# Values of the first two heads from the raw input in float32, with the norm's root and shift applied at read-out, in one step of a hybrid attention / mLSTM backbone

## The chip, the cores and the metric

The kernel runs on one core of a Trainium2 chip. The metric is device microseconds for one execution; three timed executions of the kernel before gave 2232.55, 2234.36 and 2235.95 us, median 2234.36. The engines are named as the profile names them: PE (matrix products), PEld (its weight loads), DVE, ACT and POOL (elementwise work), SP (which issues DMA transfers). L98 is line 98 of the kernel.

## The reference, cut to what matters

One layer is computed for 128 context tokens and 1024 latent tokens, 1152 in all, 1024 channels wide. Only its first stage is touched:

```
sh1, sc1, ... = adaln(cond, w_mod, b_mod)          # silu(cond) @ w_mod + b_mod; one set for the
h = rmsnorm(x, g_norm_mix) * (1.0 + sc1) + sh1     # context tokens, another for the latent ones
z = h @ w_in                                       # z is then split into q, kv, gates, values ...
mv = zmv.reshape(B, S, MLSTM_HEADS, MLSTM_DV)      # values: 4 heads of 256 columns
```

With r the reciprocal root of a token's mean square and A = g (1 + sc1) per channel, h = r x A + sh1. So a token's values can be had as h @ W, or as r (x @ (A W)) + sh1 @ W. Everything is float32.

## The kernel before, in words

Tokens lie in the columns: the input x is held as eight slices k of 128 channels, each in two halves j of 576 tokens; the 1152 tokens are also nine chunks c of 128. Chunk 0 holds the context tokens; chunk 4 lies across the two halves, and is copied together for the split products by `copy4`. Float32 products that matter are made of three products of a split operand (`mm3`, L98 to L100: high by high, high by low, low by high), after ACT has written the high part (`hi`, L69) and DVE the difference (`lo`, L75). Float32 products without a split are used where they are small.

`start` (L329 to L541) makes the normed and modulated h and the values of all heads, before `z_lat` begins the other projections from combinations of h (`t_ops`, L547 onward, makes those on POOL, ACT and DVE in the background). In order:

- `gemv` (L353): for three blocks of 256 channels, silu(c) times a block of `w_mod`, as eight float32 products with a stationary operand of two columns, then a transposition by four small products, then DVE writes shift `mod1` and scale `A1`. The last two channel slices get theirs by `row`: products and sums of rows on DVE, POOL and ACT.
- `stats` and `xr`: sum of squares per token (ACT and DVE), the reciprocal root by PE and DVE, spread over the partitions, and x times it, on DVE and POOL.
- `modk`: scale and shift (ACT for half 0, DVE for half 1), then the high and low parts.
- `vmm`: the values of one head are 256 columns, six chunks GA in the six PSUM banks named mm, then the three of GB. For each chunk and slice k three products of 256 columns, with the chunk of h stationary. `vout` copies a chunk's 256 columns out and stores them.

Each engine works through its own list of instructions in order. The lists come from the program's order by a scheduler that moves instructions by its own estimates. SP's list holds all loads and stores of this stage; a DMA whose buffer is not free holds up those behind it. Weights go through four buffers `wr` (raw) and four `wo` (high and low parts).

## Time and profile before

| what | value |
|---|---|
| median of 3 runs | 2234.36 us |
| the profiled execution | 2234.02 us |
| span of its trace (first to last instruction) | 2232.2 us |
| mean granted PE clock | 0.964 |
| PE busy | 2067.2 us (93%) |
| PEld busy | 1902.9 us (85%) |
| DVE busy | 1541.2 us (69%) |
| POOL busy | 1012.8 us (45%) |
| ACT busy | 927.0 us (42%) |

The page gives busy shares of the whole span, and then the span in forty slices of 55.8 us; the first three slices and a third of the fourth are `start`. A row of the timeline has a start, a time, the engine, the line, what is written from what, shapes and the number of instructions merged; the bracket is the idle time before it and what ended it. A PE product's time in a row is its latency; successive products overlap, so that their rate is read from starts or from merged rows. An unsplit float32 product is recorded as two.

### The profile page before, as it was taken

To read this page: it belongs to the slowest core of one execution; us is meant where nothing else is said; L and a number is where in the kernel's file an instruction comes from. 1 tells how busy PE (TensorE), PEld (TensorE's weight loads), DVE (VectorE), ACT (ScalarE), POOL (GpSimd) and SP (SyncE) were. 2 spreads that over 40 slices of the span, in tenths; PEclk is the share of its full clock that TensorE was granted. 3 is DMA by queue.
4 is the path that set the end of the run, shared out by engine and by line. 5 is a ranking of instruction groups with operands and counts; after the bars stand their busy time and mean duration, and the time that the engine had idled before them with its cause. 6 is when DMAs were issued, how large, how long until landed. Compare 5 with 4: busy or idle time off the path is not lost.

```text
span 2232.2 us, 37660 instructions
## 1 busy us (share of the span) xinstructions
PE 2067.2 (93%) x13913; PEld 1902.9 (85%) x13913; DVE 1541.2 (69%) x2710; ACT 927.0 (42%) x1846; POOL 1012.8 (45%) x754
## 2 busy tenths in 40 slices
PE   5799998999979987999999999889999999989897
PEld 1799998999978874667676799879999999989897
DVE  6735745988845877655665547899645555799895
ACT  4232333545545654333433335444322222356464
POOL 3712122767723523444445534677766634431501
PEclk8799999999999998999999999899999999999899
DMA  7221243555569876222224564224555522557664
GB/s 284 66 93 60 73 152 122 166 182 167 168 214 327 256 222 211 85 73 69 75 78 125 172 214 141 97 90 131 168 183 166 177 87 79 162 174 249 220 196 132
DMA packets 235671, 340.82 MB, mean 153 GB/s; under 512 B 20286, under 2 KB 171550, under 8 KB 234462
## 3 DMA queue, kind: packets, MB, share of 16 engines
q1 hardware_dynamic: 226942, 328.73, 46.3%
q0 software_dynamic: 4848, 6.06, 1.1%
q10 hardware_dynamic: 3696, 3.61, 0.5%
q8 instruction: 110, 1.80, 0.3%
q14 instruction: 75, 0.61, 0.1%
HBM read 250.55 MB, written 87.80 MB: 152 GB/s over the span
## 4 chain that ended last, share of the span: by engine, by line
PE 45%; DVE 12%; DMA 8%; POOL 6%; issue 5%; ACT 2%; SPq 1%; DVEq 0%; POOLq 0%; ACTq 0%
PE mm L98 11%; PE mm L100 11%; PE mm L99 10%; DVE wo L75 4%; DMA pr<-w_fo 3%; PE pv L1455 3%; PE st L98 2%; PE st L99 1%; PE st L100 1%; PE mx L1377 1%; DVE sm L1379 1%; PE p L1081 1%; POOL ps L1755 1%; POOL ps L1752 1%; POOL wm L701 1%
## 5 line engine op out<-in xcount | busy, mean ns | idle before, releaser
L100 PE MATMUL mm<-th,wo 128*128 128x288 f32 x1840 | 547.8, 298 | 14.5 <-DVE wo L75 14.2
L98 PE MATMUL mm<-th,wo 128*128 128x288 f32 x1840 | 548.9, 298 | 6.1 <-ACT m L1693 2.8
L99 PE MATMUL mm<-tl,wo 128*128 128x288 f32 x1840 | 547.3, 298 | 0.0
L100 PEld LDWEIGHTS mm<-th,wo 128*128 128x128 f32 x1840 | 349.9, 190 | 18.5 <-DVE wo L75 18.0
L75 DVE TENSOR_TENSOR wo<-wr,wo 128x512 fp32r<-128x512 f32 (+1 forms) x317 | 313.7, 1005 | 64.0 <-ACT wo L69 59.5
L98 PEld LDWEIGHTS mm<-th,wo 128*128 128x128 f32 x1840 | 349.0, 190 | 8.6 <-ACT m L1693 3.0
L99 PEld LDWEIGHTS mm<-tl,wo 128*128 128x128 f32 x1840 | 349.4, 190 | 0.1
L69 ACT ACTIVATE wo<-wr 128x512 fp32r<-128x512 f32 (+1 forms) x317 | 187.3, 608 | 147.6 <-PE mm L100 70.5
L75 DVE TENSOR_TENSOR wo<-ws,wo 128x512 fp32r<-128x512 f32 x188 | 185.8, 991 | 68.4 <-ACT wo L69 68.3
L69 ACT ACTIVATE wo<-ws 128x512 fp32r<-128x512 f32 x188 | 116.7, 627 | 276.4 <-PE mm L100 147.3
L1424 POOL TENSOR_TENSOR es<-es,p 128x512 f32<-128x512 f32 x112 | 157.3, 1404 | 91.3 <-ACT p L1417 87.4
L100 PE MATMUL mm<-xh,wo 128*128 128x288 f32 x616 | 183.5, 299 | 10.7 <-DVE wo L75 10.7
L98 PE MATMUL mm<-xh,wo 128*128 128x288 f32 x616 | 183.0, 297 | 1.2 <-ACT wo L69 1.2
L99 PE MATMUL mm<-xl,wo 128*128 128x288 f32 x616 | 183.8, 299 | 0.0
L1665 POOL TENSOR_TENSOR ws<-wr,ws 128x512 f32<-128x512 f32 x47 | 61.8, 1315 | 244.2 <-DVE wo L75 238.8
L1417 ACT ACTIVATE p<-st 128x512 f32<-128x512 f32 (+1 forms) x152 | 87.4, 578 | 157.7 <-PE st L100 146.5
L1379 DVE TENSOR_REDUCE sm<-mx 128x1 f32<-128x384 f32 (+1 forms) x200 | 99.1, 539 | 66.4 <-PE mx L1377 65.5
L98 PE MATMUL mm<-B,wo 128*128 128x288 f32 x456 | 134.8, 296 | 2.2 <-DVE zo L1681 1.3
L100 PE MATMUL mm<-B,wo 128*128 128x288 f32 x456 | 134.8, 296 | 0.0
L99 PE MATMUL mm<-B,wo 128*128 128x288 f32 x456 | 134.8, 296 | 0.0
L701 POOL TENSOR_TENSOR wm<-wm,sr 128x512 f32<-128x512 f32 x64 | 100.1, 1566 | 65.4 <-DVE mj L700 61.0
L100 PEld LDWEIGHTS mm<-xh,wo 128*128 128x128 f32 x616 | 117.2, 191 | 13.0 <-DVE wo L75 12.9
(430 smaller groups left out, 5272.7 us busy)
## 6 DMA issues: line engine op xcount, KB each, us to landing
wr<-w_ff SPq DMA_DIRECT2D x56, 512.0 KB
wm<-wm SPq DMA_DIRECT2D x32, 512.0 KB
wr<-d_w SPq DMA_DIRECT2D x32, 512.0 KB
d_z<-zo SPq DMA_DIRECT2D x48, 288.0 KB
d_g<-uu SPq DMA_DIRECT2D x44, 288.0 KB
wr<-w_big SPq DMA_DIRECT2D x24, 512.0 KB
wr<-w_fo SPq DMA_DIRECT2D x24, 512.0 KB
pr<-w_fo SPq DMA_DIRECT2D x40, 256.0 KB
```

Of the source, the lines that this page charges most:

```text
L69: i = self.nc.scalar.activation(out, in_, AF.Copy)
L75: return self.nc.vector.tensor_sub(out, in_, f32v(hi)).ins
L98: mm(out, lhs[0], rhs[0], start=first, stop=False)
L99: mm(out, lhs[0], rhs[1], start=False, stop=False)
L100: self.pe = mm(out, lhs[1], rhs[0], start=False, stop=last).ins
L701: nc.gpsimd.tensor_tensor(w[:, n], w[:, n], sr[:, 1], op=ALU.mult)
L1081: self.pe = mm(p1, A[:, h], V[:, h], start=True, stop=not carried).ins
L1379: self.iv = nc.vector.tensor_reduce(sm[:, t, j:j + 1], s[:, :kc], axis=AX.X, op=ALU.max, negate=True).ins
L1417: self.ia = nc.scalar.activation(p[:, :n], st[:, :n], AF.Exp).ins
L1424: nc.gpsimd.tensor_tensor(U["sum"], U["sum"], p, op=ALU.add)
L1455: self.pe = nc.tensor.matmul(pv[g * AV:(g + 1) * AV, q0:q0 + w], v[:, kb[c]], U["P"][c][:, q0:q0 + w], start=c < 2, stop=c == U["nc"] - 1, ...
L1665: G.tensor_tensor(s4, a12, s2, op=ALU.subtract)
```

## The change

In `start`:

- **First values from raw x.** The values of heads 0 and 1 of chunks 1 to 6 are made of x as it was loaded, unsplit, in float32 (`rawmm`), against weights that ACT multiplies by `A1` (L514). Chunk 4 is made as two products of 64 tokens each, written to the two halves of a bank's partitions, so that no copy is needed. `shift` multiplies the shift by the unscaled weights on PE (a stationary operand of 32 columns), `spread` copies the row over the partitions, and `vout` of these chunks does r times PSUM plus that row (L498).
- **Loads block by block.** Four blocks of `w_mod` (all 1024 channels) are loaded, each followed by a piece of `w_v` and two slices of x. The row products of the last two slices and their loads (`row`, `rload`, `rparams`, `sload`) are gone.
- **Modulation on column groups.** `gemv` has a stationary operand of 32 columns (two used), and four products write the four groups of 32 partitions of one bank; the sum of the groups is taken by the small products that transpose.
- **Two heads wide.** A value product has 512 columns in place of 256, and `vout` writes 512.
- **modk.** x times root and scale is one DVE instruction for slices 0 to 3 (L429), then ACT adds the shift; for slices 4 to 7 POOL multiplies by the root (L425) and ACT does scale and shift. It comes at the end of the raw products, since it overwrites x.
- The remaining values: heads 2 and 3 of GA = chunks 0 to 3, 5, 6 (while `modk` runs); then heads 0 and 1 of chunks 7, 8, 0; then heads 2 and 3 of 7, 8, 4, with `t_ops` in the background of the last two.

The instructions that follow `start` are the same on every engine, but for 25 places of PE and 16 of DVE where neighbours change places.

The first place is PE's list where the raw part ends (the names mm_209 to mm_220 are the six banks of the raw chunks; mx are the small results; wh, wl split weights; B_71, B_72 the high and low part of half 0, slices 0 to 3). Before, the split products follow the root's own small products:

```order
L280 MATMUL mm_327<-dg_324,ones 128x128 x2
L361 MATMUL mx_432<-ident,rows_430 128x2 x4
L280 MATMUL mm_334<-dg_331,ones 128x128 x2
L280 MATMUL mm_340<-dg_338,ones 128x64
L98 MATMUL mm_357<-wh_277,B_72_353 128x256
L99 MATMUL mm_357<-wl_278,B_72_353 128x256
L100 MATMUL mm_357<-wh_277,B_73_354 128x256
```

Now the same small products stand behind the last raw ones:

```order
L469 MATMUL mm_215<-ws_360,x_20_144 64x512
L473 MATMUL mm_218<-ws_360,x_20_144 128x512
L473 MATMUL mm_220<-ws_360,x_20_144 128x512
L418 MATMUL mx_397<-dg_396,ones 128x128 x4
L418 MATMUL mx_408<-dg_407,ones 128x128 x4
L418 MATMUL mx_419<-dg_418,ones 128x128
L481 MATMUL mx_459<-wr_175,shs 32x512 x2
L492 MATMUL mx_465<-shv,selr 128x512
L98 MATMUL mm_507<-wh_486,B_71_427 128x512
L99 MATMUL mm_507<-wl_487,B_71_427 128x512
L100 MATMUL mm_507<-wh_486,B_72_428 128x512
```

Between the last raw product and the first split one there are nine products that spread the root, three for the shift, and, on other engines, all that makes B.

The second place is DVE's list at that time (vs are the read-outs of raw banks, b12l the low parts of half 1, B_97 those of half 0, slices 4 to 7):

```order
L485 TENSOR_TENSOR shv<-shv,mx_459 64x512
L75 TENSOR_TENSOR B_72_428<-x_17_141,B_71_427 128x576
L75 TENSOR_TENSOR B_97_573<-x_19_143,B_96_572 128x576
L75 TENSOR_TENSOR B_72_428<-x_17_141,B_71_427 128x576 x3
L75 TENSOR_TENSOR B_97_573<-x_19_143,B_96_572 128x576
L75 TENSOR_TENSOR b12l<-x_18_142,b12h 128x576
L498 SCALAR_TENSOR_TENSOR vs_468<-mm_209,y_382,shv 128x512
L498 SCALAR_TENSOR_TENSOR vs_471<-mm_211,y_382,shv 128x512
L498 SCALAR_TENSOR_TENSOR vs_474<-mm_213,y_382,shv 128x512
L75 TENSOR_TENSOR b12l<-x_18_142,b12h 128x576
L75 TENSOR_TENSOR B_97_573<-x_19_143,B_96_572 128x576
L498 SCALAR_TENSOR_TENSOR vs_477<-mm_215,y_382,shv 128x512
```

The twelve L429 instructions stand just ahead of these rows; the first read-out of a raw bank is the twenty-first instruction, counted from the first L429.

The third place is POOL's list (t_118 is `t_ops`' first difference, c the copies for chunk 4):

```order
L425 TENSOR_TENSOR x_19_143<-x_19_143,rbc 128x576 x4
L425 TENSOR_TENSOR x_20_144<-x_20_144,rbc 128x576 x4
L443 COPY c_83_490<-B_71_427 128x4x64
L443 COPY c_83_490<-B_72_428 128x4x64
L569 TENSOR_TENSOR t_118_773<-x_18_142,x_17_141 128x2304
L443 COPY c_83_490<-B_96_572 128x4x64
L443 COPY c_83_490<-b12h 128x4x64
L443 COPY c_83_490<-B_97_573 128x4x64
L443 COPY c_83_490<-B_98_578 128x4x64
L443 COPY c_83_490<-b12l 128x4x64
L569 TENSOR_TENSOR x_18_142<-x_20_144,x_18_142 128x2304
```

Before, POOL's first difference stood behind twelve multiplications by the root and two row products; now behind eight multiplications.

The diff, cut:

```
-        def xload(j):
-            for k in range(0, KD, 2):
+        def xload(b):
+            k = 2 * b
+            for j in range(2):
...
         def gemv(b):
-            g = self.bank(pp, "mx")[0:2]
+            g = self.bank(pp, "mx")
             for k in range(KD):
-                nc.tensor.matmul(g, self.silc[:, k, :], gw[b, k // 4][:, k % 4], start=k == 0, stop=k == KD - 1)
+                j = 32 * (k % 4)
+                nc.tensor.matmul(g[j:j + 32], sil[:, k], gw[b, k // 4][:, k % 4], start=k < 4, stop=k >= 4)
...
+        GR, GA, GB, GC = (1, 2, 3, 4, 5, 6), (0, 1, 2, 3, 5, 6), (7, 8, 0), (7, 8, 4)
...
+        def square(b):
+            for k in (2 * b, 2 * b + 1):
+                for j in range(2):
+                    c = slice(j * GT, (j + 1) * GT)
+                    t = sqs[:, (2 * k + j) % 4] if k else acc[:, c]
+                    nc.scalar.activation(t, xv(k, j), AF.Square)
+                    if k:
+                        nc.vector.tensor_add(acc[:, c], acc[:, c], t)
...
         def modk(k, j):
             x = xv(k, j)
+            if k >= 4:
+                nc.gpsimd.tensor_tensor(x, x, rbc[:, j * GT:(j + 1) * GT], op=ALU.mult)
             for c, s in ((slice(0, TP), 0), (slice(TP, GT), 1)) if j == 0 else ((slice(0, GT), 1),):
...
+                if k < 4:
+                    nc.vector.scalar_tensor_tensor(x[:, c], x[:, c], A, rbc[:, j * GT + c.start:j * GT + c.stop], op0=ALU.mult, op1=ALU.mult)
+                    nc.scalar.activation(x[:, c], x[:, c], AF.Identity, bias=sh)
                 else:
+                    nc.scalar.activation(x[:, c], x[:, c], AF.Identity, bias=sh, scale=A)
...
+        def rawmm(b, sw):
+            w = sw.rearrange("p (k f) -> p k f", k=2)
+            for e in range(2):
+                k = 2 * b + e
+                for c in GR:
+                    if k == 0:
+                        ps[c] = self.bank(pp, "mm")
+                    if c == 4:
+                        for j, t in ((0, slice(GT - 64, GT)), (1, slice(0, 64))):
+                            nc.tensor.matmul(ps[c][64 * j:64 * j + 64], xv(k, j)[:, t], w[:, e], start=k == 0, stop=k == KD - 1,
+                                             skip_group_check=True)
+                    else:
+                        j, t = c // 4, c * P - (c // 4) * GT
+                        nc.tensor.matmul(ps[c], xv(k, j)[:, t:t + P], w[:, e], start=k == 0, stop=k == KD - 1)
+        def shift(b):
+            g = self.bank(pp, "mx")
+            for e in range(2):
+                nc.tensor.matmul(g[32 * e:32 * e + 32], shs[:, 2 * b + e], raw[b][:, 512 * e:512 * e + 512], start=True, stop=True)
...
+        def vout(hp, c, r=None, sh=None):
+            vs = vp.tile([P, 2 * DV], F32, name=self.nm("vs"), tag="vs", bufs=3)
+            if r is not None:
+                nc.vector.scalar_tensor_tensor(vs, ps[c], r[:, c:c + 1], sh, op0=ALU.mult, op1=ALU.add)
...
+        for b in range(4):
+            block(b)
+            vload(b)
+            xload(b)
+        for b in range(4):
+            gemv(b)
+            sw = f32v(self.wp.tile([P, 4 * DV], R32, name=self.nm("ws"), tag="wo", bufs=self.wb[1]))
+            for e in range(2):
+                k = 2 * b + e
+                nc.scalar.activation(sw[:, 512 * e:512 * e + 512], raw[b][:, 512 * e:512 * e + 512], AF.Copy, scale=self.A1[:, k, 1:2])
+            square(b)
+            if b == 3:
+                r = stats()
+                for k in range(2):
+                    for j in range(2):
+                        modk(k, j)
+            rawmm(b, sw)
+            shift(b)
...
+        spread()
+        for c in GR:
+            vout(0, c, r, shv)
```

More of the change, by code (lines that the diff above doesn't have):

```diff
@@ L360, in gemv @@
             for f in range(4):
-                nc.tensor.matmul(pm[:, f, :], rows[:, f * P:(f + 1) * P], self.ident[0:2, 0:2], start=True, stop=True)
+                nc.tensor.matmul(pm[:, f, :], rows[:, f * P:(f + 1) * P], self.vec[:, self.V_SEL:self.V_SEL + 2], start=True, stop=True)
             for s in range(2):
@@ new lines, in stats @@
+        def stats():
+            st = self.bank(pp, "mx")
+            for c in range(NCH):
+                nc.tensor.matmul(st[:, c:c + 1], acc[:, c * P:(c + 1) * P], self.ones[:, 0:1], start=True, stop=True)
+            r = self.rsqrt(st[:, :NCH], NCH, D, sp)
+            for c0, n in ((0, 4), (4, 4), (8, 1)):
+                dg = sp.tile([P, 4, P], F32, name=self.nm("dg"), tag="dg", bufs=2)
+                bc = self.bank(pp, "mx")
+                for i in range(n):
+                    nc.vector.tensor_scalar(dg[:, i, :], self.ident, r[:, c0 + i:c0 + i + 1], None, op0=ALU.mult)
+                    nc.tensor.matmul(bc[:, i * P:(i + 1) * P], self.ones, dg[:, i], start=True, stop=True)
+                nc.scalar.copy(rbc[:, c0 * P:(c0 + n) * P], bc[:, :n * P])
+            return r
```

209 lines of the change are left out of this document (79 added, 130 removed).

## The prediction

> **What bounds the kernel now.** I read the page's slices first (PE busy, and the clock granted to it, in tenths), then the first 300 us in stretches, then the timeline at both ends of the values.
>
> ```profile
> PE   5799998999979987999999999889999999989897
> ...
> PEclk8799999999999998999999999899999999999899
> ```
>
> The slices that fall furthest short are the first two: that is `start`.
>
> ```profile
> 0.00:10.00 10.00, 3.77 (x5) 0.57 (x6) 0.00 (x0) 1.50 (x2) 0.84 (x7) 1.00 0.82 304
> 10.00:20.00 10.00, 7.22 (x30) 3.00 (x28) 7.89 (x17) 8.72 (x14) 0.00 (x0) 0.99 1.04 392
> 20.00:30.00 10.00, 5.48 (x7) 0.85 (x8) 6.51 (x21) 3.20 (x5) 0.00 (x0) 0.50 1.03 423
> 30.00:40.00 10.00, 7.86 (x39) 4.02 (x38) 5.66 (x6) 6.82 (x12) 7.44 (x5) 1.00 0.88 357
> 40.00:60.00 20.00, 12.62 (x33) 5.11 (x33) 19.05 (x40) 7.17 (x13) 10.28 (x4) 0.76 0.31 106
> 60.00:96.00 36.00, 27.13 (x174) 26.05 (x174) 33.37 (x31) 14.20 (x26) 31.94 (x17) 0.75 0.15 48
> 96.00:112.00 16.00, 12.80 (x92) 12.40 (x92) 5.24 (x2) 1.65 (x3) 7.16 (x2) 0.89 0.18 57
> 112.00:184.00 72.00, 72.00 (x602) 72.00 (x602) 19.76 (x22) 19.21 (x25) 6.09 (x3) 1.00 0.26 83
> ...
> 184.00:300.00 116.00, 116.00 (x893) 116.00 (x893) 80.81 (x160) 38.80 (x82) 27.27 (x20) 1.00 0.29 97
> ```
>
> Columns: stretch, its length, busy us of PE, PEld, DVE, ACT, POOL, granted clock, DMA share, GB/s. Up to 40 us the loads run at full rate and PE does small things. From 60 to 96 PE is busy 27 of 36 us at 0.75 of its clock, while DVE is busy 33.4 and POOL 31.9. From 112 on PE never stops, and it does not stop in the next stage either. So until 112 the normed and modulated operands set the pace, behind that PE, and what `start` gains finds no slack at 184 in which to vanish.
>
> ```profile
> 60.27 0.56 PE L98 MATMUL mm<-wh,B 128*128 128x256 f32 x1
> ...
> 184.06 0.28 PE L98 MATMUL mm<-wh,c 128*128 128x256 f32 x1
> 184.18 0.28 PE L99 MATMUL mm<-wl,c 128*128 128x256 f32 x1
> 184.30 0.28 PE L100 MATMUL mm<-wh,c 128*128 128x256 f32 x1
> 184.42 0.30 PE L98 MATMUL mm<-B,wo 128*128 128x288 f32 x1
> ```
>
> These are the first value product, the last three, and the first of the next stage at 184.4. Value products start 0.12 us apart; 4 heads x 9 chunks x 8 slices x 3 = 864 of them need 103.7 us and took 124.1. So 60 us lie ahead of the values, and 20 us of stall and half clock within.
>
> **The change part by part.** The sum is a new time for the first product behind `start`, to be held against 184.4.
>
> *Start of the raw products.* Block 0 is 2 x 1024 KB of `w_mod`, 512 KB of `w_v` and 2 x 576 KB of x, 3.8 MB. The first ten us of the trace move 3.04 MB, the next at 392 GB/s, so it has landed at 10 + 0.76/0.39 = 11.9 us.
>
> ```profile
> 11.58 1.26 ACT L155 ACTIVATE sq<-x 128x576 f32<-128x576 f32 x2 [0.25 <-DMA x<-xT]
> ...
> 15.40 0.56 ACT L358 COPY rows<-mx 2x512 f32<-2x512 f32 x1
> ...
> 16.10 1.02 PE L361 MATMUL mx<-ident,rows 2*128 2x2 f32 x8 [1.18 <-ACT rows L358]
> ...
> 17.28 0.23 DVE L364 TENSOR_TENSOR mod<-mx,bm 128x4 f32<-128x4 f32 x2
> ...
> 18.67 0.35 DVE L366 TENSOR_SCALAR A<-mod,vec 128x2 f32<-128x2 f32 x2
> ```
>
> The last pair of squares (1.26) stands ahead of the scaling in ACT's list; then one scaling of 512 weights, about 0.6 by L155's rate; 0.7 for handovers: 14.5 us. DVE's small operations for `A1` lie beside the squares. Later blocks need 3.8/0.4 = 9.5 us each and PE some 14 (below), so loading is hidden; had PE only the 10.3 us of products, it would still be. The remaining `w_v` pieces wait in SP's list for raw buffers, and three of them behind the six stores of raw chunks, which wait for read-outs; PE wants those three over 30 us after these stores, so that costs nothing.
>
> *The raw products.*
>
> ```profile
> 32.45 3.59 PE L356 MATMUL mx<-wm,silc 128*2 128x512 f32 x8
> ...
> L1455 PE MATMUL pv<-p,v x352: 221/592/1116, 868.1 to 1247.1; 128*64 128x512 f32 x128, 128*64 128x256 f32 x32, 128*64 128x64 f32 x16
> ...
> 868.62 1.46 PE L1455 MATMUL pv<-p,v 128*64 128x512 f32 x6
> 870.01 0.50 PE L98 MATMUL st<-q,k 97*128 97x512 f32 x1
> ...
> 870.57 0.40 PE L100 MATMUL st<-q,k 97*128 97x512 f32 x1
> 870.80 0.40 PE L98 MATMUL st<-q,k 97*128 97x512 f32 x1
> ```
>
> The first row is four unsplit products of 512 columns, eight records, in 3.59 us: a record each 0.43 us, a product 0.86. The attention's L1455 writes the two halves of a bank from stationary operands of 64 columns. Its median latency is 0.59, and six records took 1.46 us. One behind the other they would have taken 5 x 0.43 + 0.59 = 2.74; two at a time 2 x 0.43 + 0.59 = 1.45. So products to different column groups run side by side. A slice then costs five chunks and the pair of chunk 4, 6 x 0.86 = 5.2 us, and eight slices 41.3. They replace 288 split products of 256 columns, 34.6 us: PE has more to do here, but can begin 46 us earlier, since only the scale has to be known and not the root.
>
> *gemv, shift, and the gaps between blocks.* Four groups at once are in no row, two are. Bounds for the eight products of a gemv: 1.7 us with four at once, 6.9 in a row. I take 1.7, as the pair shows no loss at all. From block 0 to 1 the path is gemv 1.7, copy 0.6, four small products 0.5, DVE 0.7, then in PE's list the shift's pair (0.86) and the next gemv (1.7) ahead of the raw products, beside which the scaling lies: 6.1 us. Afterwards the gemv is done beforehand: 0.5 + 0.7 + 0.86 + 1.7 = 3.8, and in the last gap nine products for the root and 0.5 of waiting, 2.1: 12 us in all. Where PE idles the clock is halved (0.50 from 20 to 30 us); for the first block I add 1.5 us, between 0 and the 5 of half clock throughout. The raw part ends at 14.5 + 41.3 + 12 + 1.5 = 69.3 us.
>
> The Trainium skill ("TensorE: Matmul & The Clock Gate", Part 3: Packing small matmuls) states 2.38x for three column groups of 32; at that share of the ideal four give, as an estimate, a gemv of 2.2 us and a sum 2 us later; no row here has such groups. The Trainium skill ("TensorEngine Tiling (Array Packing)", Key Properties) says that changing the tiling mode drains TensorE: the product behind the attention's pair took 0.50 and the later ones 0.40, so the trace agrees at 0.1 us a change; some 32 changes of the raw part would make the sum 3 us later.
>
> *The bubble.* The first split product needs one of the six banks, so a read-out; it is the twenty-first DVE instruction from the first L429, and needs the root spread over the partitions and the spread shift.
>
> ```profile
> 30.80 1.33 PE L280 MATMUL mm<-dg,ones 128*128 128x128 f32 x10
> ...
> 60.79 2.66 DVE L423 TENSOR_TENSOR x<-x,ar 128x576 f32<-128x576 f32 x2
> 60.84 10.37 POOL L423 TENSOR_TENSOR x<-x,ar 128x576 f32<-128x576 f32 x6 [8.71 <-ACT ar L281]
> ...
> 62.42 2.17 ACT L430 ACTIVATE x<-x,mod,A 128x128 f32<-128x128 f32 x4
> ...
> 72.22 6.68 POOL L547 TENSOR_TENSOR t<-x,x 128x2304 f32<-128x2304 f32 x1 [1.02 <-DVE x L428]
> ...
> 82.80 0.75 DVE L75 TENSOR_TENSOR b12l<-x,b12h 128x576 fp32r<-128x576 f32 x1
> 83.47 8.98 DVE L75 TENSOR_TENSOR B<-x,B 128x576 fp32r<-128x576 f32 x5
> ...
> 85.31 5.65 POOL L547 TENSOR_TENSOR x<-x,x 128x2304 f32<-128x2304 f32 x1
> ...
> 98.13 5.11 POOL L547 TENSOR_TENSOR t<-x,x 128x2304 f32<-128x2304 f32 x1
> ```
>
> Here DVE and POOL hold each other up: a DVE difference of 0.75 starts 0.67 before the next one, but five of them took 8.98 us across one POOL instruction of 5.65, and two multiplications took 2.66 while POOL did its own. POOL needs 5.11 for 2304 elements where DVE is idle, so 1.3 for 576; with DVE at work six took 10.37, 1.73 each. They take turns. From the last raw product: four spreading products 1.1 (ten records in 1.33), a copy 0.56, and both once more, so the root is there at 2.8. Then POOL's eight multiplications in turn with DVE's eight large L429 (priced like differences): 8 x (1.3 + 0.67) = 15.8, to 18.6. The shift's sum 0.6, seven differences 4.7 and 0.8 for POOL's copies between, one read-out 0.6: the first split product 25 us behind the raw ones. Low bound: without turns DVE's chain ends at 2.8 + 5.4 + 0.6 + 4.7 + 0.6 = 14, but ACT has some 27 instructions ahead of the spread shift, 0.54 each by L430's four, and ends near 17. High bound: one difference of POOL (6.68) and its successor (5.65) get in ahead of the read-outs: 37. The middle value is nearest to the rows from 60 to 71 us, which are the same two engines on the same tiles.
>
> *The rest.* The last two attention rows start 0.23 apart: 512 columns cost 0.23 against 2 x 0.12. The 144 products of GA take 33.1 us, and I add 3.4 for the clock that the bubble halves (0.75 from 60 to 96 us). The sixth read-out stands behind three more differences and POOL's first L569, at about 36, which is about when PE comes to that bank; the last low part comes near 45 and is needed near 57. Then 144 products of the last six chunks, 33.1. Each 18 of them (4.1 us) cover one split of weights on ACT and DVE and a share of `t_ops`, as in the 72 us of full PE before; without that cover it would cost up to 1 us in each of eight pieces.
>
> Sum: 69.3 + 25 + 3.4 + 66.2 = 163.9 against 184.4, so 20.5 us less. The span becomes 2211.7; the profiled execution has 1.8 us beyond its span, so 2213.5, and it stands 0.3 below the median of the runs. The row products, their loads and half of the read-outs that go are paid for inside this sum.
>
> **The rivals.**
>
> *Light bubble.* DVE's L429 is not held up by POOL, ACT sets 17 us, and the raw part has no half clock: 8 + 1.5 us more gained, 30 in all, 2204. For it: L429 is another operation than those held up in the rows. Against it: it reads two tensors as they do.
>
> *Heavy bubble.* POOL's two differences come between low parts and read-outs, 37 us in place of 25: 8.5 us less than before, 2225. For it: the first difference stands directly behind the first copies in POOL's list. Against it: by then DVE is past all but the second half of its low parts.
>
> *Column groups in turn.* If products of 32 columns to different groups queue up after all, a gemv costs 5.2 us more, four 20.6; with chunk 4's second halves (8 x 0.86) and the shift's (4 x 0.86) the loss is 31 us: 2213.5 + 31 = 2244, slower than before. It decides from a loss of 20.5 us on, so the gemv alone suffices. Against it: L1455's pairs. For it: four moving operands at once are in no row.
>
> *Given back.* The next stage starts earlier, but finds `t_ops` unfinished, squeezed from 72 us into 33: no change, 2234. Against it: POOL's four differences are 5.1 to 6.7 us each, 24 in sum, and two of them fit into GA.
>
> **How the numbers follow.** Forecast 0.60 (its own range 2205 to 2221: a bubble of 19 to 31 us and 2 us each way in the raw part), light bubble 0.18, heavy 0.11, given back 0.06, column groups in turn 0.05. The range, 2197 to 2229, holds the first three, below 2204 for a bubble that also leaves the clock alone (3.4) and 3.6 for the raw part's gaps. Past 0.2%, 4.5 us, about the least that a measurement of this kernel can tell from no change: faster 0.88, same 0.07, slower 0.05.
>
> **What would show it.** Right: raw products of 0.43 us a record from about 14.5 to 69 us; a gemv of 16 records in about 2 us; one gap of PE that ends near 94 with the read-out L498 as its releaser; the next stage's first product near 164; nothing changed behind it. Wrong: a gemv of over 5 us, raw products that wait for x, a gap of over 45 us, or a next stage that starts early and stalls.

## The result and the profile after

The changed kernel takes 2214.5 us (median; 2213.69 to 2219.35) beside 2234.69 us of the kernel before on the same chip: a ratio of 0.9915, with a 95% interval of 0.9898 to 0.9932. The profiled execution took 2214.21 us, of which its span is 2212.4. The forecast was 2213.5 us, faster, within 2197 to 2229.

The slices of the page, PE's busy share and the clock granted to it, in the changed kernel:

```profile
PE   8699989999979988999999899889999999989897
...
PEclk9899999999999997999999999899999999999998
```

The first two were 5 and 7 before and are 8 and 6 now: PE works in the first 55 us and stands still later, between the raw and the split products. The timeline of PE shows that in full; of four raw blocks the first two are given (columns: start, length from the first start to the last end, engine, line, operation, tiles, count of records, and in brackets the idle time ahead and its releaser):

```profile
7.49 3.64 PE L367 MATMUL mx<-wm,sil 128*32 128x512 f32 x16 [7.49 <-ACT sil L380]
11.84 1.87 PE L372 MATMUL mx<-vec,rows 128*128 128x2 f32 x8 [0.70 <-ACT rows L369]
14.82 1.92 PE L481 MATMUL mx<-wr,shs 128*32 128x512 f32 x4 [1.11 <-issue]
16.67 4.18 PE L473 MATMUL mm<-ws,x 128*128 128x512 f32 x6
...
29.21 1.92 PE L367 MATMUL mx<-wm,sil 128*32 128x512 f32 x16
...
36.09 2.84 PE L473 MATMUL mm<-ws,x 128*128 128x512 f32 x6
38.86 1.08 PE L469 MATMUL mm<-ws,x 128*64 128x512 f32 x4
39.87 4.56 PE L473 MATMUL mm<-ws,x 128*128 128x512 f32 x10
44.36 1.08 PE L469 MATMUL mm<-ws,x 128*64 128x512 f32 x4
...
76.34 2.29 PE L418 MATMUL mx<-dg,ones 128*128 128x128 f32 x18
...
94.42 2.04 PE L492 MATMUL mx<-shv,selr 64*128 64x512 f32 x2 [14.40 <-DVE shv L485]
99.67 0.79 PE L98 MATMUL mm<-wh,B 128*128 128x512 f32 x1 [3.21 <-DVE vs L498]
...
167.50 0.29 PE L98 MATMUL mm<-B,wo 128*128 128x288 f32 x1
```

Raw products run from 16.67 to 76.3, the first split product starts at 99.67, and the next stage at 167.50, where it started at 184.42 before: 16.9 us earlier. The other 2.9 of the span's 19.8 us are won behind `start`, where the instructions are the same; more on them below.

In the stretch between, 23.3 us long, PE waits for DVE. (DVE is also called VectorE below, ACT ScalarE and POOL GpSimd.) DVE's timeline there:

```profile
78.05 15.63 DVE L429 SCALAR_TENSOR_TENSOR x<-x,A,rbc 128x128 f32<-128x128 f32 x12
93.60 0.67 DVE L485 TENSOR_TENSOR shv<-shv,mx 64x512 f32<-64x512 f32 x1
94.20 4.08 DVE L75 TENSOR_TENSOR B<-x,B 128x576 fp32r<-128x576 f32 x6
98.21 0.74 DVE L75 TENSOR_TENSOR b12l<-x,b12h 128x576 fp32r<-128x576 f32 x1
98.88 2.05 DVE L498 SCALAR_TENSOR_TENSOR vs<-mm,y,shv 128x512 f32<-128x512 f32 x3
100.86 4.06 DVE L75 TENSOR_TENSOR b12l<-x,b12h 128x576 fp32r<-128x576 f32 x1
...
109.78 7.92 DVE L75 TENSOR_TENSOR B<-x,B 128x576 fp32r<-128x576 f32 x4
```

Twelve multiplications with the root in 15.63 us, the shift's sum, seven low parts, then the first read-out. Six equal low parts take 4.08 us at 94.20, one takes 4.06 at 100.86 and four 7.92 at 109.78: the latter lie beside GpSimd's differences. GpSimd's own timeline:

```profile
79.00 14.07 POOL L425 TENSOR_TENSOR x<-x,rbc 128x576 f32<-128x576 f32 x8 [77.08 <-ACT rbc L419]
...
99.18 5.12 POOL L569 TENSOR_TENSOR t<-x,x 128x2304 f32<-128x2304 f32 x1
...
110.76 5.66 POOL L569 TENSOR_TENSOR x<-x,x 128x2304 f32<-128x2304 f32 x1
```

Behind 112 us PE is full, as the busy times by stretch show (columns as in the prediction):

```profile
76.30:99.60 23.30, 5.43 (x25) 2.70 (x23) 22.97 (x24) 19.52 (x36) 16.62 (x11) 0.67 0.14 45
99.60:112.00 12.40, 12.33 (x44) 10.00 (x45) 12.40 (x14) 5.16 (x9) 9.27 (x7) 0.79 0.34 127
112.00:167.50 55.50, 55.50 (x246) 45.83 (x245) 37.67 (x22) 22.88 (x22) 20.71 (x7) 1.00 0.42 138
```

### The profile page after: what moved, and what is told of

Its sections match the earlier page's. It is cut to its first block, busy times and chain, and to the rows that moved or that the text cites. A ratio compares the mean times of both kernels' runs of the same rounds, so it can differ in the third digit from the quotient of the medians.

```text
span 2212.4 us, 36762 instructions
## 1 busy us (share of the span) xinstructions
PE 2057.7 (93%) x13487; PEld 1864.7 (84%) x13487; DVE 1537.4 (69%) x2690; ACT 932.1 (42%) x1848; POOL 999.2 (45%) x750
## 4 chain that ended last, share of the span: by engine, by line
PE 43%; DVE 11%; DMA 7%; POOL 4%; issue 4%; ACT 2%; SPq 1%; DVEq 0%; POOLq 0%; ACTq 0%
PE mm L98 10%; PE mm L100 10%; PE mm L99 10%; DVE wo L75 3%; PE pv L1477 3%; DMA pr<-w_fo 2%; PE st L98 2%; PE st L99 1%; PE st L100 1%; PE mx L1399 1%; DVE sm L1401 1%; DMA S<-d_s 1%; PE p L1103 1%; POOL ps L1774 1%; PE p L1108 1%
## 5 line engine op out<-in xcount | busy, mean ns | idle before, releaser
L100 PE MATMUL mm<-th,wo 128*128 128x288 f32 x1840 | 547.5, 298 | 14.2 <-DVE wo L75 13.9
L100 PE MATMUL mm<-xh,wo 128*128 128x288 f32 x616 | 183.4, 299 | 10.6 <-DVE wo L75 10.6
```

The source lines that it names most:

```text
L100: self.pe = mm(out, lhs[1], rhs[0], start=False, stop=last).ins
```

## The experiments

My theory was the prediction's: column groups run side by side; the raw part fills the loading time; the 23 us behind it come from DVE and GpSimd holding each other up in a queue that puts read-outs last; from there PE sets the pace. The rivals: groups run in turn or don't matter; the raw part loses behind itself what it gains; the 23 us are DVE's own work; something other than PE sets the pace later. "Next stage" in the table is the start of its first product in the profiled execution; the ratio is to the kernel before, on the same chip.

| kernel | median us | ratio, 95% interval | next stage at |
|---|---|---|---|
| changed kernel | 2214.5 | 0.9915 (0.9898 to 0.9932) | 167.50 |
| one_group | 2234.63 | 1.0004 (0.9990 to 1.0019) | 186.94 |
| tiny_pool | 2209.18 | 0.9889 (0.9866 to 0.9912) | 165.54 |
| no_raw | 2222.36 | 0.9947 (0.9927 to 0.9967) | 174.05 |
| early | 2205.69 | 0.9871 (0.9852 to 0.9891) | 159.97 |
| inturn | 2203.99 | 0.9864 (0.9843 to 0.9885) | 156.59 |
| inturn2 | 2196.63 | 0.9834 (0.9820 to 0.9847) | 149.75 |
| whole_c4 | 2219.87 | 0.9940 (0.9920 to 0.9961) | 167.10 |
| cols256 | 2220.48 | 0.9939 (0.9916 to 0.9962) | 172.35 |
| late_diff | 2216.15 | 0.9926 (0.9912 to 0.9940) | 172.97 |

### Are the column groups worth anything?

```diff
-                j = 32 * (k % 4)
-                nc.tensor.matmul(g[j:j + 32], sil[:, k], gw[b, k // 4][:, k % 4], start=k < 4, stop=k >= 4)
+                nc.tensor.matmul(g[0:32], sil[:, k], gw[b, k // 4][:, k % 4], start=k == 0, stop=k == KD - 1)
```

> Everything is as in the changed kernel, but the eight products of a block of the modulation (L367) all go into one column group, one after the other. Theory A (the four column groups run side by side): sixteen records took 1.92 us in the changed kernel; in turn they take 16 x 0.43 = 6.9 us, 5.0 more in each of the four blocks, and the first block, at half clock, up to 10 more. The gaps ahead of the raw products hold them, so the next stage starts 15 to 25 us later: 2230 to 2240 us. Rival B (the products run in turn as it is, or the modulation is hidden behind the loads of x): a record is no shorter or its length no matter, and the time stays within 3 us of 2214.5.

One column group takes 7.0 us for sixteen records, as this row of PE's timeline shows, against 1.92 for the four groups of the changed kernel:

```profile
41.16 7.03 PE L366 MATMUL mx<-wm,sil 128*32 128x512 f32 x16
...
186.94 0.29 PE L98 MATMUL mm<-B,wo 128*128 128x288 f32 x1
```

The next stage starts 19.4 us later and the whole gain over the kernel before is gone: theory A. Without the column groups of the gemv the rest of the change would have brought nothing.

### What does GpSimd cost DVE?

```diff
-                nc.gpsimd.tensor_tensor(x, x, rbc[:, j * GT:(j + 1) * GT], op=ALU.mult)
+                nc.gpsimd.tensor_tensor(x[:, 0:8], x[:, 0:8], rbc[:, j * GT:j * GT + 8], op=ALU.mult)
```

> GpSimd's multiplications with the root (L425, x of the second four k) work on 8 columns in place of 576; the rest of those columns is left without the root, so values and everything behind them differ. What waits for what stays. Theory A (DVE and GpSimd hold each other up while both read two tensors): DVE's twelve L429, 15.6 us in the changed kernel, fall to some 8 to 9 us (0.76 us for 576 columns, as the sums at L405 take), the first read-out starts 5 to 8 us earlier after the last raw product than the 22.6 us of now, and the time is 2206 to 2211 us. Rival B (1.37 us is what an L429 takes by itself): L429 stays within 10%, the gap stays at 22 to 24 us, the time within 2 us of 2214.5.

The groups of DVE from 76 to 93 us in tiny_pool (mean in ns behind the busy time), whose last raw product ends at 76.9:

```profile
L429 DVE SCALAR_TENSOR_TENSOR x<-x,A,rbc 128x128 f32<-128x128 f32 (+2 forms) x12 | 6.5, 612 | 0.0
```

The same twelve instructions had a mean of 1375 ns in the changed kernel, so more than half of their time was waiting for GpSimd. The first read-out starts at 91.64, 14.7 us behind the raw products in place of 22.5, and the time lies in A's range; its interval still touches that of the changed kernel, so it is the row that decides. Rival B falls: 1.37 us is not what an L429 takes by itself. early, below, confirms the price with every value right: there the twelve L429 (55.12 to 61.56) run while GpSimd is idle, and take 6.44 us. The Trainium skill ("SBUF — State Buffer", SBUF: two separate sides) describes an exclusive lock between a VectorE operation with two inputs from SBUF and a GpSimd operation, held for a whole instruction; these rows agree, and the prediction's turn-taking is this lock.

Of the 7.8 us that the first read-out gained, 5.4 reach the first split product (17.9 us behind the raw ones in place of 23.3) and only 2.0 the next stage. Two more rows of tiny_pool, DVE's and PE's, show where some of it went:

```profile
94.29 5.12 DVE L75 TENSOR_TENSOR B<-x,B 128x576 fp32r<-128x576 f32 x1 [0.58 <-ACT B L69]
...
100.12 0.80 PE L98 MATMUL mm<-wh,B 128*128 128x512 f32 x1 [2.38 <-DVE vs L498]
```

GpSimd's first difference (93.69 to 98.79) now gets in ahead of the fourth read-out; a low part takes 5.12 us beside it, the read-out starts at 99.33, and PE stands still for 2.4 us: the prediction's heavy bubble, in small. The median fell by 5.3 us, more than this trace accounts for.

### Is it the raw part at all?

no_raw drops `sw`, `rawmm`, `shift` and `spread` and makes all four heads' values from the split input:

```diff
-        order = [(0, GR, kk) for kk in range(4)] + [(hp, g, kk) for hp, g in ((1, GA), (0, GB), (1, GC)) for kk in range(4)]
+        order = [(hp, g, kk) for hp, g in ((0, GA), (0, GC), (1, GA), (1, GC)) for kk in range(4)]
```

> The first part of the change alone is undone: no value is made from the raw input. All of them are products of the split, modulated input, 432 of 512 columns, for chunks in two groups for each pair of heads; the modulation on column groups and the values two heads wide stay. Theory A (what counts is that PE has work while the root is made): the split products start when the first k is modulated, about as early as the first raw part ends or somewhat before, and 432 x 0.227 = 98 us of them follow, DVE's 6 us a k setting the pace of the first eight: the next stage starts at 175 to 185, against 167.5, and the time is 2221 to 2232 us. Rival B (the raw part gives nothing: what it saves in products is lost again in the 23 us without any between it and the split ones): 2211 to 2217 us. Rival C (the raw part is the whole of the gain or more): 2233 us and above.

The first split product in no_raw's timeline of PE:

```profile
58.31 0.80 PE L98 MATMUL mm<-wh,B 128*128 128x512 f32 x1 [4.54 <-ACT B L69]
```

The busy times of the stretches that follow it, in the same kernel:

```profile
60.00:80.00 20.00, 12.43 (x43) 9.21 (x43) 20.00 (x14) 17.32 (x29) 17.98 (x10) 0.77 0.00 0
80.00:100.00 20.00, 16.11 (x61) 12.77 (x61) 13.12 (x10) 2.70 (x3) 16.10 (x8) 0.83 0.17 53
100.00:120.00 20.00, 20.00 (x90) 16.57 (x89) 11.18 (x8) 8.03 (x8) 3.70 (x1) 1.00 0.49 157
```

Split products begin at 58.3, 41 us earlier than in the changed kernel, but from 60 to 100 us PE is busy 28.5 of 40 us, at 0.77 and 0.83 of its clock, while DVE, busy 33 of them, and GpSimd, 34, still prepare the operands. The next stage starts 6.6 us later than with the raw part, and 10.4 earlier than before the change. So A: the time is inside its range, the start of the next stage 1 us ahead of its own. Of the 20 us some 11 are there without the raw part, which adds 7 to 8 (the two intervals still overlap, from 0.9927 to 0.9932; the start of the next stage points the same way).

### Where the 23 us go when the root is made early

The raw part needs no root, but nothing forces the root to wait for its end either. early loads all of x ahead of the last two modulation blocks and moves four calls:

```diff
-            xload(b)
+            for n in ((0, 1), (2, 3), (), ())[b]:
+                xload(n)
...
-            square(b)
-            if b == 3:
-                r = stats()
-                for k in range(2):
-                    for j in range(2):
-                        modk(k, j)
-            rawmm(b, sw)
             shift(b)
+            if b == 3:
+                spread()
+            rawmm(b, sw)
+            if b == 1:
+                r = stats()
+            for k in ((), (0,), (1, 2, 3), ())[b]:
+                for j in range(2):
+                    modk(k, j)
```

(with `square` of blocks 0, 1 and 2, 3 at the first two b, and `modk` of the other four k inside the split products).

> The raw part stays, but the root no longer waits for its end: all of x is loaded ahead of the last two blocks of modulation weights, all squares are taken in the first two blocks, the root is made behind the second block of raw products, the multiplications with it for the first four k run beside the third and fourth, and the shift is spread ahead of the fourth block's products. What is computed is the same. Theory A (the 23 us without products behind the raw part come from the root's place in the order and the queue of DVE, nothing else): the split products follow the raw ones within 3 us, at full clock, and the time falls by 15 to 22 us: 2193 to 2200. Rival B (DVE, ACT and GpSimd need those 23 us anyhow, and slow the raw part's own gaps by as much): within 4 us of 2214.5. Rival C (the next stage is bound by its own loads and sums, so it starts no earlier): the products end early and the time falls by less than 5 us.

PE's timeline in early, around the third and fourth raw block and the end:

```profile
56.03 1.92 PE L367 MATMUL mx<-wm,sil 128*32 128x512 f32 x16 [0.41 <-ACT rbc L419]
59.53 1.05 PE L372 MATMUL mx<-vec,rows 128*128 128x2 f32 x8 [1.57 <-ACT rows L369]
63.22 1.07 PE L481 MATMUL mx<-wr,shs 128*32 128x512 f32 x2 [2.63 <-issue]
...
92.82 1.98 PE L473 MATMUL mm<-ws,x 128*128 128x512 f32 x4
94.24 0.79 PE L98 MATMUL mm<-wh,B 128*128 128x512 f32 x1
...
159.97 0.29 PE L98 MATMUL mm<-B,wo 128*128 128x288 f32 x1
```

The first split product follows the raw ones without a pause, so the 23 us did come from the order, as A says. But the raw part ends at 94.2 instead of 76.3: its three gaps grew from 13.9 to 28.5 us (10.7, 15.0 and 2.8), and the first two blocks to 13 us each by half clock. The rows show the second gap, 53.41 to 68.44. The third gemv waits 0.4 us for a bank that the root's spreading holds. Its transposes wait for the copy of its rows, which ScalarE makes at 58.91, behind instructions of the modulation. The shift's products wait for VectorE, which takes up the transposed rows at 62.15, behind the twelve L429 (6.44 us) and a low part. Then the shift and the fourth gemv run at half clock (0.51 granted) until 68.44; the scaled weights, which queue behind ScalarE's modulation until 66.60, come just before that. In the first gap the products that sum the squares, 4.00 us from 36.40, stand ahead of the raw ones. The time fell by 9 us, between A's 15 to 22 and B's nothing: A on the cause of the 23 us, B on what it costs elsewhere. Rival C falls: the next stage starts 7.5 us earlier, and follows the last split product at once.

### Putting the gaps in order

inturn writes out PE's order in the raw part (each group of products is told to stand behind the one before) and splits `gemv` into its products and its transposes:

```diff
+        part(1, 1, GR[2:])
+        inturn(gemv_p, 2)
+        inturn(stats_b)
+        inturn(gemv_t, 2)
+        scaled(2)
...
+        part(2, 0)
+        inturn(shift, 2)
+        part(2, 1, GR[:2])
+        inturn(gemv_p, 3)
+        part(2, 1, GR[2:])
+        inturn(gemv_t, 3)
+        scaled(3)
```

`part(b, e)` is half a block of `rawmm`, `gemv_p` and `gemv_t` the products and the transposes of `gemv`, `scaled` the scaling of its weights, `stats_b` the spreading of the root.

> The step behind the early root: the same early loads of x and early root, and PE's own order around the raw blocks is written out, so that the products of each next modulation block stand inside the raw products of the one before, its transposes behind them, and the scaling of its weights ahead of the squares and of the root's multiplications on ScalarE and VectorE. What is computed is the same. Theory A (the 14 us that the early root gave back lay in the gaps between raw blocks, where scaled weights waited behind squares, root and difference work): the raw part ends at 74 to 80 instead of 94, the split products follow at once, the next stage starts at 141 to 148 instead of 160, and the time is 2190 to 2197 us. Rival B (the loads or the engines' total work set the raw part's end): it ends at 88 or later and the time stays at 2201 to 2208. Rival C (the next stage is held by its own inputs, GpSimd's differences above all): the products end early, and the time is 2198 to 2203.

The raw part ends at 88.9, and the time is not told apart from early's. Two timelines of inturn name what held the last gap open. DVE's:

```profile
66.86 5.60 DVE L75 TENSOR_TENSOR b12l<-x,b12h 128x576 fp32r<-128x576 f32 x1
72.38 0.94 DVE L75 TENSOR_TENSOR B<-x,B 128x576 fp32r<-128x576 f32 x1
...
73.92 0.22 DVE L382 TENSOR_TENSOR mod<-mx,bm 128x4 f32<-128x4 f32 x2
```

GpSimd's:

```profile
66.27 5.57 POOL L639 TENSOR_TENSOR t<-x,x 128x2304 f32<-128x2304 f32 x1
```

The first of `t_ops`' differences for the next stage had moved up between GpSimd's modulation work. One low part of 0.75 us took 5.60 beside it, and the modulation of the fourth block (L382), which PE's raw products wait for, stood behind that low part. So B's numbers came out, but not its cause, as inturn2 shows: it is the queue again, at another place. inturn2 puts it elsewhere:

```diff
-        sub = lambda o, x, y: G.tensor_tensor(o, x, y, op=ALU.subtract)
+        def sub(o, x, y):
+            with self.tc.issue_after(self.c4last):
+                G.tensor_tensor(o, x, y, op=ALU.subtract)
...
-            self.lo(l[:, k % 4], x, h[:, k % 4])
+            with self.tc.issue_after(self.gv):
+                self.lo(l[:, k % 4], x, h[:, k % 4])
...
+        part(1, 1, GR[2:4])
+        inturn(gemv_p, 2)
+        part(1, 1, GR[4:])
+        inturn(gemv_t, 2)
+        scaled(2)
+        inturn(stats_b)
...
+        part(2, 0)
+        inturn(gemv_p, 3)
+        part(2, 1, GR[:3])
+        inturn(shift, 2)
+        inturn(gemv_t, 3)
+        scaled(3)
+        part(2, 1, GR[3:])
```

(`c4last` is GpSimd's last copy for chunk 4, `gv` the last DVE instruction of the latest modulation block.)

> As the run with PE's own order written out, with what its trace showed still standing in the way put elsewhere: the products and transposes of the fourth modulation block stand deeper inside the third block of raw products; the transposes of the third ahead of the spreading of the root; GpSimd's first difference over 2304 columns (5.6 us, in which VectorE's next low part took 5.6 too, with the fourth block's modulation queued behind it) goes behind all of GpSimd's own modulation work; the low parts go behind the modulation of the block at hand. What is computed is the same. Theory A (these two gaps of 7.2 and 6.2 us between raw blocks were queueing): they fall to 4 and 1.5, the raw part ends at 78 to 82 instead of 88.9, the next stage starts at 146 to 150 instead of 156.6, and the time is 2193 to 2199 us. Rival B (the delay moves on to the first split products, whose difference work is now later): the next stage starts at 153 or later, 2201 to 2206 us.

PE's timeline of inturn2, the last raw products and what follows:

```profile
69.48 1.05 PE L494 MATMUL mx<-wr,shs 128*32 128x512 f32 x4
70.47 2.84 PE L486 MATMUL mm<-ws,x 128*128 128x512 f32 x6
...
81.00 1.98 PE L486 MATMUL mm<-ws,x 128*128 128x512 f32 x4
82.42 0.79 PE L98 MATMUL mm<-wh,B 128*128 128x512 f32 x1
...
149.75 0.29 PE L98 MATMUL mm<-B,wo 128*128 128x288 f32 x1
```

The gap ahead of the fourth block is one pair of shift products, the one ahead of the third 3.7 us; the split products follow at once at 82.4, and the next stage at 149.75, 34.7 us earlier than before the change: A, though the raw part ends just past A's 82. The edit moves four things at once, so what each of them brought is not shown. At 2196.63 us this version computes what the changed kernel, early and inturn compute, and is faster than all three, by 18 us than the changed kernel.

### Two sizes that the sum had wrong or left open

whole_c4 makes chunk 4 of the raw part with one product of 128 columns over the first half of x, and so leaves that chunk's values wrong:

```diff
-                        for j, t in ((0, slice(GT - 64, GT)), (1, slice(0, 64))):
-                            nc.tensor.matmul(ps[c][64 * j:64 * j + 64], xv(k, j)[:, t], w[:, e], start=k == 0, stop=k == KD - 1,
-                                             skip_group_check=True)
+                        nc.tensor.matmul(ps[c], xv(k, 0)[:, GT - P:GT], w[:, e], start=k == 0, stop=k == KD - 1)
```

> The changed kernel, with the raw products of the chunk that lies across both halves of x as one product over 128 columns of the first half in place of two over 64 columns side by side: that chunk's values are left wrong, everything else and all that waits is as it was. Theory A (a raw block takes 11.1 us where 10.3 was forecast because PE drains at each of the four changes between products of 128 and of 64 columns, some 0.1 us each, the rest being 0.44 for a record where I took 0.43): a block takes 24 x 0.44 = 10.6 us, 0.5 less, and the time falls by 1 to 3 us. Rival B (two products of 64 columns run only partly side by side and cost more than one of 128): a block takes 10.0 to 10.3, and the time falls by 3 to 5 us. Rival C (neither; the matrix is always loaded at this pace): no change within 0.2 us a block.

Its second raw block, as PE's timeline has it:

```profile
37.70 2.84 PE L471 MATMUL mm<-ws,x 128*128 128x512 f32 x6
40.37 1.02 PE L468 MATMUL mm<-ws,x 128*128 128x512 f32 x2
41.23 4.46 PE L471 MATMUL mm<-ws,x 128*128 128x512 f32 x10
45.52 1.02 PE L468 MATMUL mm<-ws,x 128*128 128x512 f32 x2
...
48.10 0.95 PE L372 MATMUL mx<-vec,rows 128*128 128x2 f32 x8
```

10.40 us from the first raw product to what follows, against 11.10 for the same block of the changed kernel, and 4.29 us for ten records (41.23 to 45.52), 0.43 each. So my 0.43 for a record was right and A's 0.44 wrong; all of the surplus comes with the pairs of 64 columns. Taking both rows apart, a pair's successor starts 1.01 us behind it where that of a product of 128 starts 0.86 behind, and the other products beside a pair lose 0.1 at each change of form: 0.35 us a pair. The size lies between A's (10.6) and B's (at most 10.3). The 2.8 us of four blocks are not to be seen in the time: the median is 5.4 us above the changed kernel's, where A and B both had it lower, with intervals that overlap. In the trace the half clock lasted longer (0.55 granted from 33.89 to 37.70, where the changed kernel has 1.00) and the second block began 1.6 us later, so the next stage starts only 0.4 us earlier; why the median is higher is not shown. What this run decides is the length of a block, not the time.

cols256 gives the split products two halves of 256 columns again:

```diff
-            self.mm3(ps[c], hc(k, c), (w[0][:, k % 2], w[1][:, k % 2]), k == 0, k == KD - 1)
+            x, mm = hc(k, c), nc.tensor.matmul
+            for n, (l, r) in enumerate(((0, 0), (0, 1), (1, 0))):
+                ends = k == 0 and n == 0, k == KD - 1 and n == 2
+                for s in (slice(0, 512),) if any(ends) else (slice(0, DV), slice(DV, 512)):
+                    i = mm(ps[c][:, s], x[l], w[r][:, k % 2, s], start=ends[0], stop=ends[1])
+            self.pe = i.ins
```

> The changed kernel with its split products 256 columns wide again, as before the change: two products in place of one, but for the first and the last of each of the eighteen sums of 24 (the first clears the whole bank). What is computed is the same. In place of 288 products of 512 columns there are 24 of 512 and 528 of 256. By the pitches of the traces (0.227 and 0.120 us) PE needs 24 x 0.227 + 528 x 0.120 = 68.8 us in place of 65.4. Theory A (PE sets the pace behind the read-outs): 2 to 4 us more, 2216 to 2219. Rival B (the sums and splits of weights on VectorE, ScalarE and GpSimd set it): within 1 us of 2214.5. Rival C (values two heads wide bring more than their products, because read-outs and loads of weights are what counts): nothing is lost here, as B, and the gain of that part lies in the halved number of read-outs.

The stretch from the first split product (99.81) to the next stage in cols256:

```profile
99.80:172.30 72.50, 71.93 (x552) 70.22 (x553) 45.32 (x34) 28.07 (x31) 30.01 (x13) 0.96 0.37 128
```

72.5 us where the changed kernel needs 67.8, with PE busy throughout: 4.7 more, some over the 3.4 by the pitches. The time, 6 us more, is above A's range by 1.5 us, and its interval overlaps the changed kernel's; by the trace it is A, PE sets the pace here, and B and C fall. (The expectation's eighteen sums are twelve: 288 products in sums of 24. Its counts of 24 and 528 are right.)

### Do the differences behind the read-outs cost anything?

late_diff moves `t_ops`' differences in the changed kernel behind GpSimd's last copy (`sub` as in inturn2) and nothing else.

> The changed kernel with one thing moved: GpSimd's four differences over 2304 columns (the first two stood between its copies, at 99 and 111 us) go behind the last of its copies; VectorE's order is the same. Theory A (GpSimd and VectorE hold each other up, and PE waits for VectorE until about 112): the two low parts that took 4.1 us, and part of 7.9 for four, behind those differences take 0.7 each, VectorE's last low part comes 6 to 9 us earlier, PE no longer idles behind the first split product, and the time falls by 1 to 4 us, to 2210 to 2213. Rival B (PE is bound by its own half clock there, and by the read-outs): low parts are earlier but the next stage is not, the time within 1 us of 2214.5. Rival C (the differences come late for the next stage): 2 us or more slower.

DVE's timeline of late_diff, the low parts behind the first read-outs:

```profile
104.48 0.74 DVE L75 TENSOR_TENSOR b12l<-x,b12h 128x576 fp32r<-128x576 f32 x1
...
109.80 2.75 DVE L75 TENSOR_TENSOR B<-x,B 128x576 fp32r<-128x576 f32 x4
```

These are the low parts that took 4.06 and 7.92 us. The last of them ends 9 us behind the first split product (103.29) instead of 18, as A has it, and yet the next stage starts 69.7 us behind that product rather than 67.8, and the time is 1.6 us more, which its interval does not tell from none. So B in its mechanism, though its 1 us is missed by 0.6: behind the read-outs PE has the operands in time anyway. A's premise does not hold in the changed kernel either: PE is busy for 12.33 of the 12.33 us from 99.67 to 112, at a granted clock of 0.79. C is there in small: 1.2 of the 1.9 us are a wait of PE at 144.94 for the low part of a weight on DVE, where an earlier one (131.75) had taken 5.40 us beside GpSimd's last difference (130.91 to 136.07). The lock costs time only where PE's next operand is the one that is held.

## Why the prediction was right, point by point

The forecast of 2213.5 us missed by 1.0 us, but parts of it were off by more, and in both directions. Against the sum's 163.9 for the next stage's first product the trace has 167.5.

- *Start of the raw products*, 14.5 predicted, 16.67 measured: +2.2. About half of it is the scaling. The last piece of x for block 0 came at 13.6 and not at 11.9 (ACT's square at 13.63 waits for that DMA), and the modulation's scale at 14.9, behind transposes that take 1.87 us here and 1.05 in later blocks; so the first scaled weights were done at 15.60. The other half is a step left out: the shift's products (L481) stand ahead of the raw ones in PE's list in the first block too, and at half pace (1.85 us) they held PE until 16.67.
- *The raw products*, 41.3 predicted; four blocks of 11.1 are 44.4: +3.1. The failing step is "the pair shows no loss at all": the pair costs 0.35 us more than one product, eight pairs 2.8. The attention's six records from which I took it were one pair after another, with no change of form between them. The Trainium skill ("TensorEngine Tiling (Array Packing)", Key Properties), which I had weighed and set aside, has the drain at such changes; the rows agree with it, at 0.1 us a change. The estimate of 3 us that I had worked out from it was the nearer one, in part by coincidence: it counted some 32 changes, where the eight pairs make 16 (1.6 us), and the other 1.2 us are the 0.15 that each pair takes longer than one product.
- *Gaps*, 6.1 + 3.8 + 2.1 = 12 predicted, 6.89, 4.15 and 2.82 measured: +1.9. The transposes (L372) take 1.05 us a block and not 0.5. That gemvs of later blocks are done ahead was right; so were the gemv's 1.7 us (1.92 to the end of the last), which one_group shows to be worth the 20.6 us that the rival gave it (20.1 in the time).
- *Half clock in the first block*, 1.5 predicted, 1.4 measured: a first block of 12.5 in place of 11.1. That this was half clock is inferred from the pace: the granted clock reads 1.00 there, but 0.50 in early and late_diff, where the same shift products take the same 1.85 us.
- *The bubble*, 25 predicted, 23.3 measured: -1.7. The mechanism was right and is shown by tiny_pool; the order of DVE was as forecast, L429 done at 93.6, seven low parts in 4.7. The root was there 1.7 us behind the raw products and not 2.8, and GpSimd's copies (0.8) fell beside something else. One reading under the price was wrong: where POOL took 5.11 us for 2304 elements, DVE was not idle but held, in a low part of a weight that took 4.91 us there (99.41 in the kernel before) and takes 1.22 elsewhere. The price stands all the same: late_diff has 5.16 (113.47), with DVE idle from 112.55 to 117.47.
- *Behind it*, 69.6 predicted, 67.8 measured: -1.8. The pitch was 0.2275 us, so 65.5 for 288, and 2.3 for the half clock rather than 3.4. That PE sets the pace here is what cols256 and late_diff show.

These add up to +3.6 us. Of that, 2.9 came back behind `start`, so that the time came out nearly as forecast: this is luck, and its cause stays open. The experiments' times and starts of the next stage disagree by as much: against the kernel before, late_diff gains 11.5 us at that start and 18.1 in the time, whole_c4 17.3 and 13.8, though the instructions behind `start` are the same ones but for a few places. From the next stage's start to the end of the span, with these instructions, the eleven traces took from 2038.4 to 2049.9 us. A single profiled execution therefore tells no cause of 3 us in the whole. In the raw part one cause of such differences can be seen: in late_diff, whose products there are those of the changed kernel, 14 records of the third gemv took 3.76 us in place of 2.18 and the first six raw records of the fourth block 4.47 in place of 2.82, at a granted clock of 0.57 and 0.62 where the changed kernel has 1.00, and the raw part ended 3.6 us later.

Of the rivals, the light bubble falls by L429's 1375 ns; the heavy one too, as GpSimd's first difference starts at 99.18, behind the first read-out's start; column groups in turn is what one_group makes of the kernel, and not what the kernel does; nothing is given back, since the next stage follows the last split product without waiting. What the prediction did not see is how much of the forecast bubble was avoidable: its length was taken as a cost of the raw part, where it was the price of where the root stands in the program.

## What to carry to other kernels

Work that needs no result of a slow chain should run beside that chain, not ahead of it: against the version without a raw part, the kernel gained 8 us from a raw part that the root followed, and 26 when, besides, the root was made beside it and the small work between blocks was put into the right places of each engine's list. (No run has that order without the raw part, so the 26 us are not shown to be the raw part's.) When a stall vanishes, look at once at what now stands in those lists ahead of the work that the waiting engine needs next: here twice the gain went into other gaps, and each time a row of DVE or ScalarE named the culprit. A GpSimd elementwise operation on large tiles stopped VectorE's operations with two SBUF inputs for nearly its whole length, while read-outs, with one of their two tensors in PSUM, went on beside it (three in 2.05 us from 98.88 in the changed kernel); so put it where VectorE's next low part or product is not urgent.

## What the runs showed of the hardware that I had not expected

Four column groups of 32 run with no loss that the rows could show: sixteen records in 1.92 us against 7.03 in one group, 1.3 against 6.5 from first start to last. The Trainium skill ("TensorE: Matmul & The Clock Gate", Part 3: Packing small matmuls) states 2.38x for three groups, 0.79 of the ideal; four groups here bring 3.7x (7.03 to 1.92), 0.92 of it, and the measurement decides. A pair of products of 64 columns among products of 128, on the other hand, costs 0.35 us over a whole one. And VectorE's hold by GpSimd is nearly total: 0.75 us of work took 5.60 us beside a GpSimd instruction of 5.57.
